# Seven-product pairs in the second round of both FFN down projections, and a weight stream that loads by free tiles

## The chip, the cores and the metric

The kernel runs on one core of one Trainium2 chip. The metric is the device time of one execution in microseconds (us), as the median of three runs. Engines are called as the profile calls them: PE (TensorE matmul), PEld (its weight loads), DVE (VectorE), ACT (ScalarE), POOL (GpSimd), SP (SyncE, which here only issues DMAs).

## The reference, cut to what matters

The program is a two-layer decoder trunk over 512 tokens of width 1024: a Mamba-2 layer, an FFN, a latent attention layer, a second FFN, with a layer norm after each of the four. The change sits in the FFN, which runs twice:

```python
def conv_ffn(h, up, conv_w, conv_b, down):
    u = causal_depthwise_conv(h @ up, conv_w, conv_b)
    g, val = jnp.split(u, 2, axis=-1)
    return (jax.nn.silu(g) * val) @ down
...
        h = layer_norm(DN_ALPHA * h + mix, ln_mix_g[i], ln_mix_b[i])
        ff = conv_ffn(h, ffn_up[i], ffn_conv_w[i], ffn_conv_b[i], ffn_down[i])
        h = layer_norm(DN_ALPHA * h + ff, ln_ffn_g[i], ln_ffn_b[i])
```

`up` is 1024 x 5632 and `down` 2816 x 1024, both float32. The hidden width of 2816 is 22 tiles of 128.

## The kernel before

**Precision.** Every large product is made of three float32r matmuls: each operand is split into a rounded part and a remainder (`h` and `l`), and hh, hl and lh are added up in PSUM (`mm_a` for the up projection, lines 148, `mm_b` for the down projection, lines 154 to 156). A weight tile therefore goes through three steps before PE can use it: a DMA into a staging tile `wst`, a cast on ACT into `wh` (line 84), and a subtraction on DVE into `wl` (line 85). The last two are called a split here. An item of the stream is one such tile, 128 x 1024 (wide) or 128 x 512 (narrow).

**The weight stream.** `WStream` walks a list of items made ahead of time. There are 3 staging tiles and 6 pairs of `wh` and `wl`. `get(i)` splits items up to 4 ahead of `i`, never more than 6 beyond the last item retired; after each split the stream issues loads until 3 items past the split are loaded. SP issues its DMAs in the written order; a DMA whose staging tile is still in use holds up those behind it. DVE and ACT also take their instructions in a fixed order, made by a scheduler from program order and its own estimate.

**The FFN** (function `ffn`) works in two rounds over the hidden tiles. Round 0 takes tiles 0 to 9, round 1 tiles 10 to 21. A round first makes its hidden tiles: for each tile 48 matmuls (gate and value), then convolution, silu, gate on ACT and DVE (`conv3_silu_gate`). Then it multiplies them by their rows of `down`:

- Round 0 takes the tiles in pairs of an even and an odd one (`down_pairs`). With two halves of the tokens and two halves of the output columns, one pair is a 2 x 2 by 2 x 2 block product, which is done with seven block products in place of eight. `pair_operands` makes the four sums of hidden tiles on DVE; the sums of the weights are made in three `sums` tiles (`rs`, `rs2`). The item kinds say how: "r" loads into the sum, "a" is a DMA from POOL that adds to it, "+" adds a staged tile to it on DVE (line 78), "=" uses that same staged tile by itself, "-" subtracts a staged tile from the sum (line 81). The seven products run in the order a11, s1, then s2 and s4 alternating, s3, a12, a22, into PSUM banks X, Y and Z (two banks each, one for each of two token tiles). After a product, `add` moves its banks into the residual `h` on DVE (line 341), since X and Y are used again.
- The five pairs of round 0 are cut into parts of two, two and one pairs, one item for each part: 21 items a round.
- Round 1 takes its 12 tiles in the plain way: for the first half of the columns all four token tiles at once over 6 wide items, then for the second half one token tile after the other over 6 more, with the layer norm of a token tile behind its last product. In the last FFN the last token tile's second half is made in two quarters, so that its layer norm (`ln_last`) starts early.

The layer norm's parameters (`lngb`, 1 MB) share their place with the sums, and are loaded by SP after round 0.

Of the kernel before, what the change touches and what calls it, by code (L numbers as in the profile page):

```python
# [18 lines left out]
P = 128  # L19
# [11 lines left out]
class WStream:  # L31
    def __init__(self, k, items, nb, nst, la):
        self.k, self.items, self.nb, self.nst, self.la = k, items, nb, nst, la
        self.loaded = 0
        self.split = 0
        self.done = 0
        self.st = {}
        self.w = {}

    def _load(self):  # L40

        i = self.loaded
        src, f, kind, part = (self.items[i] + (None, None))[:4]
        if kind == "=":
            self.st[i] = self.st[i - 1]
            self.loaded += 1
            return  # L50
        if kind in ("r", "a"):
            t = self.sums[part]
            v = t[:, :f].rearrange("p (a n) -> p a n", a=src.shape[1])
            if kind == "r":
                self.k.nc.sync.dma_start(v, src)
            else:
                self.k.nc.gpsimd.dma_start(v, src, accum_op=ALU.add)
            self.st[i] = t
            self.loaded += 1
            return  # L60
        t = self.k.wst.tile([P, 1024], F32, name="wst")
# [3 lines left out]
        self.k.nc.sync.dma_start(dst, src)  # L65
        self.st[i] = t
        self.loaded += 1

    def _split(self, nst=None):
        nc = self.k.nc  # L70
        i = self.split
        while self.loaded <= i:
            self._load()
        f, kind, part = (self.items[i][1:] + (None, None))[:3]
        s = self.st.pop(i)
        if kind == "+":
            r = self.sums[part]
            nc.vector.tensor_tensor(r[:, :f], r[:, :f], s[:, :f], op=ALU.add)
            s = r
        elif kind == "-":  # L80
            nc.vector.tensor_tensor(s[:, :f], self.sums[part][:, :f], s[:, :f], op=ALU.subtract)
        h = self.k.wh.tile([P, 1024], F32R, name="wh")
        l = self.k.wl.tile([P, 1024], F32R, name="wl")
        nc.scalar.copy(h[:, :f], s[:, :f])  # L84
        nc.vector.tensor_tensor(l[:, :f], s[:, :f], h[:, :f], op=ALU.subtract)  # L85
        self.w[i] = (h, l)
        self.split += 1
        while self.loaded < min(len(self.items), self.split + (self.nst if nst is None else nst)):
            self._load()
# [17 lines left out]
class K:  # L107
    def __init__(self, tc, ctx, nb=6, nst=3, la=4):
        self.tc, self.nc, self.ctx = tc, tc.nc, ctx
        nc = self.nc  # L110
        self.nb, self.nst, self.la = nb, nst, la
        pool = lambda n, b, **kw: ctx.enter_context(tc.tile_pool(name=n, bufs=b, **kw))

        self.small = pool("small", 1)
        self.const = pool("const", 1)
        self.hp = pool("hp", 1)
        self.htp = pool("htp", 1)
        self.wst = pool("wst", nst)
# [12 lines left out]
        self.st = {}  # L131
# [114 lines left out]
R0 = 10  # L246


def ffn_items(up, down):


    it = []
    dv = down.rearrange("(k p) n -> p k n", p=P)
    for r in range(2):
        ks = range(R0) if r == 0 else range(R0, HT)
        for c in ks:
            it.append((up[c], 1024))
            it.append((up[c + HT], 1024))
        if r:
            for hf in range(2):  # L260
                for j in range(R0, HT, 2):
                    it.append((dv[:, j:j + 2, hf * 512:(hf + 1) * 512], 1024))
            continue

        def b(odd, hf, j):
            n = min(4, R0 - j)
            return dv[:, j:j + n, hf * 512:(hf + 1) * 512].rearrange("p (k e) n -> p k e n", e=2)[:, :, odd, :], n * 256

        for odd, hf, kinds in ((0, 0, "r"), (0, 1, "a"), (1, 1, "+="), (0, 0, "-"), (1, 0, None), (1, 0, "a")):
            for p, j in enumerate(range(0, R0, 4)):  # L270
                for kind in kinds or (None,):
                    it.append(b(odd, hf, j) + (kind, p))
# [43 lines left out]
def down_pairs(k, ws, n, prs):  # L316
# [6 lines left out]
    ni = (len(prs) + 1) // 2  # L323
    seen = set()

    def product(bs, op, p, i, start, stop):
        wh, wl = ws.get(i)
        ps = prs[2 * p:2 * p + 2]
# [8 lines left out]
    def add(bs, row, hf, sign):  # L337
        for t in range(2):
            i = 2 * row + t
            hs = k.h[:, i, hf * 512:(hf + 1) * 512]  # L340
            last = nc.vector.scalar_tensor_tensor(hs, hs, 1.0 if (i, hf) in seen else ALPHA, bs[t], op0=ALU.mult,  # L341
                                                  op1=ALU.add if sign > 0 else ALU.subtract)
            seen.add((i, hf))
# [29 lines left out]
def ffn(k, ws, base, cwp, gb, la=2, out=None, mid=None):  # L373

    nc, tc = k.nc, k.tc
    with ExitStack() as c:
# [6 lines left out]

        rs = k.lnp.tile([P, 2, DM], F32, name="rs", tag="lngb")
        ws.sums = [rs[:, 0], rs[:, 1], pools["rs"].tile([P, 512], F32, name="rs2")]
        new_gt = lambda: pools["gt"].tile([P, 2, SEQ], F32R, name="gt")
        for r in range(2):
            gts, prs, half = [], [], {}

            def finish(ci, bg, bv):  # L390
                if r:
# [7 lines left out]
                j = ci // 2  # L399
# [43 lines left out]
            for hf in range(2):  # L443
                final = hf == 1
                nk = HT - R0
                if not final:
                    bs = [k.bank() for _ in range(NT)]
                    for j in range(0, nk, 2):
                        wh, wl = ws.get(n)
                        for jj in range(2):  # L450
                            for i in range(NT):
                                k.mm_b(bs[i], gts[j + jj], slice(i * P, (i + 1) * P), wh[:, jj * 512:(jj + 1) * 512],
                                       wl[:, jj * 512:(jj + 1) * 512], j + jj == 0, j + jj == nk - 1)
                        ws.retire(n)
                        n += 1
                    ws.ahead(n)
                    for i in range(NT):
                        k.add_mix(i, hf, bs[i], 1.0, True)
                else:
                    if out is None:  # L460
                        k.new_ht()
                    def piece(i, b, c0, c1, retire):
                        for jc in range(6):
                            wh, wl = ws.get(n + jc)
                            for jj in range(2):
                                j = jc * 2 + jj
                                o = slice(jj * 512 + c0, jj * 512 + c1)
                                k.mm_b(b, gts[j], slice(i * P, (i + 1) * P), wh[:, o], wl[:, o], j == 0, j == nk - 1)
                            if retire:
                                ws.retire(n + jc)  # L470

                    for i in range(NT):
                        if out is not None and i == NT - 1:
                            bs = [k.bank(), k.bank()]
                            for e in range(2):
                                piece(i, bs[e][:, :256], e * 256, e * 256 + 256, e == 1)
                            k.ln_last(i, [v[:, :256] for v in bs], out[i * P:(i + 1) * P, :])
                            continue
                        b = k.bank()
                        piece(i, b, 0, 512, i == NT - 1)  # L480
                        if i == NT - 1:
                            ws.ahead(n + 6, la)
                        k.add_mix(i, hf, b, 1.0, True)
                        if out is None and i:
                            k.transpose_h(i - 1)
                        k.ln_apply(i)
                        if out is not None:
                            for f in range(2):
                                fs = slice(f * 512, (f + 1) * 512)
                                nc.sync.dma_start(out[i * P:(i + 1) * P, fs], k.h[:, i, fs])  # L490
                    n += 6
# [31 lines left out]
def ssd(k, ws, base, xT, x, cwp, hv, ngp, gb):  # L523
    nc, tc = k.nc, k.tc
    with ExitStack() as cx:
# [28 lines left out]
        ws.loaded = 1  # L554
        for a, e in XT:
# [6 lines left out]
            elif e < KT:  # L562
                ws._load()
# [729 lines left out]
def trunk_kernel(tc, *aps):  # L1293
    d = dict(zip(_INS, aps))
    out = aps[len(_INS)]
    with ExitStack() as ctx:
# [6 lines left out]
        ws = WStream(k, items, k.nb, k.nst, k.la)  # L1303
# [57 lines left out]
```

## Time and profile before

| what | value |
|---|---|
| median of 3 runs | 1334.68 us (1333.44 to 1335.08) |
| the profiled execution | 1332.25 us, of which its span is 1330.5 us |
| granted PE clock | 0.999 |
| first FFN: up of round 0, its products, up of round 1, its down | from 434.3, 535.8, 585.1, 715.7 to 782.8 us |
| second FFN: the same stages | from 976.1, 1077.6, 1126.8, 1257.3 to 1323.0 us |
| DMA traffic | 140.39 MB, mean 106 GB/s |

The profile shows one execution. Its span is the time from the first to the last instruction; some 1.8 us of the execution lie around it. Instruction rows give the start, the duration, engine, line and the tiles, then in brackets how long the engine sat idle before and what released it. Matmuls are pipelined, so the duration of one is longer than the time from its start to the next one's.

### The profile page before, as it was taken

To read this page: it belongs to the slowest core of one execution; us is meant where nothing else is said; L and a number is where in the kernel's file an instruction comes from. 1 tells how busy PE (TensorE), PEld (TensorE's weight loads), DVE (VectorE), ACT (ScalarE), POOL (GpSimd) and SP (SyncE) were. 2 spreads that over 40 slices of the span, in tenths; PEclk is the share of its full clock that TensorE was granted. 3 is DMA by queue.
4 is the path that set the end of the run, shared out by engine and by line. 5 is a ranking of instruction groups with operands and counts; after the bars stand their busy time and mean duration, and the time that the engine had idled before them with its cause. 6 is when DMAs were issued, how large, how long until landed. Compare 5 with 4: busy or idle time off the path is not lost.

```text
span 1330.5 us, 17374 instructions
## 1 busy us (share of the span) xinstructions
PE 1317.7 (99%) x6794; PEld 1114.5 (84%) x6794; DVE 945.3 (71%) x1433; ACT 616.7 (46%) x988; POOL 88.9 (7%) x86
## 2 busy tenths in 40 slices
PE   9999999999999999999999999999999999999997
PEld 8888888888888988788888899888898887888886
DVE  7788898788798877766664366888577786565534
ACT  6665555546443544344443144665254443444411
POOL 0111011001012001000000022000100100000001
PEclk9999999999999999999999999999999999999999
DMA  7433422332321443452223222311053426333211
GB/s 245 177 111 112 127 93 98 112 126 69 123 96 51 137 139 66 109 200 96 95 95 108 67 90 66 94 48 64 32 162 95 122 50 197 137 99 100 101 49 64
DMA packets 47186, 140.39 MB, mean 106 GB/s; under 512 B 4960, under 2 KB 5984, under 8 KB 45568
## 3 DMA queue, kind: packets, MB, share of 16 engines
q1 hardware_dynamic: 44352, 134.04, 30.5%
q0 software_dynamic: 2752, 5.24, 2.3%
q8 instruction: 53, 0.87, 0.3%
q14 instruction: 29, 0.24, 0.1%
HBM read 137.10 MB, written 2.16 MB: 105 GB/s over the span
## 4 chain that ended last, share of the span: by engine, by line
PE 95%; DVE 2%; DMA 2%; issue 1%; ACT 0%; SPq 0%; DVEq 0%; ACTq 0%
PE ps L148 57%; PE ps L154 9%; PE ps L156 9%; PE ps L155 9%; PE ps L1181 2%; PE ps L731 1%; PE ps L1215 1%; DMA wst<-in_down_dram 1%; PE ps L739 1%; DVE wl L85 1%; PE ps L234 1%; PE ps L720 1%; PE ps L698 1%; PE ps L1202 1%; PE ps L839 1%; PE ps L672 1%
## 5 line engine op out<-in xcount | busy, mean ns | idle before, releaser
L148 PE MATMUL ps<-ht,wh 128*128 128x512 f32 (+1 forms) x2272 | 518.8, 379 | 0.7 <-ACT ht L237 0.4
L148 PEld LDWEIGHTS ps<-ht,wh 128*128 128x128 f32 x2272 | 409.1, 188 | 79.8 <-ACT ht L237 0.8
L85 DVE TENSOR_TENSOR wl<-wst,wh 128x1024 fp32r<-128x1024 f32 (+3 forms) x220 | 259.8, 1188 | 99.0 <-ACT wh L84 98.7
L84 ACT CAST wh<-wst 128x1024 fp32r<-128x1024 f32 (+3 forms) x220 | 222.7, 1018 | 163.5 <-PE ps L156 88.8
L148 PE MATMUL ps<-ht,wl 128*128 128x512 f32 (+1 forms) x1136 | 267.4, 378 | 0.0
L148 PEld LDWEIGHTS ps<-ht,wl 128*128 128x128 f32 x1136 | 206.0, 188 | 39.4
L154 PE MATMUL ps<-wh,gt 128*128 128x512 f32 (+1 forms) x344 | 131.8, 383 | 2.6 <-DVE h L341 2.6
L155 PE MATMUL ps<-wl,gt 128*128 128x512 f32 (+1 forms) x344 | 131.4, 382 | 0.0
L156 PE MATMUL ps<-wh,gt 128*128 128x512 f32 (+1 forms) x344 | 131.4, 382 | 0.0
L283 DVE SCALAR_TENSOR_TENSOR acc<-ps,cw,acc 128x511 f32<-128x511 f32 x88 | 65.7, 746 | 88.6 <-ACT acc L282 88.6
L587 DVE SCALAR_TENSOR_TENSOR cv<-ps,cw,cv 128x511 f32<-128x511 f32 (+2 forms) x96 | 71.2, 744 | 34.1 <-ACT cv L585 33.5
L282 ACT ACTIVATE acc<-ps,cw 128x512 f32<-128x512 f32 x88 | 68.3, 776 | 36.8 <-PE ps L148 36.8
L295 ACT CAST gt<-acc 128x512 fp32r<-128x512 f32 (+1 forms) x64 | 36.9, 586 | 97.2 <-DVE acc L288 95.4
L154 PEld LDWEIGHTS ps<-wh,gt 128*128 128x128 f32 x344 | 64.7, 188 | 15.8 <-DVE h L341 3.5
L156 PEld LDWEIGHTS ps<-wh,gt 128*128 128x128 f32 x344 | 64.7, 188 | 12.5
L155 PEld LDWEIGHTS ps<-wl,gt 128*128 128x128 f32 x344 | 64.7, 188 | 12.4
L284 DVE SCALAR_TENSOR_TENSOR acc<-ps,cw,acc 128x510 f32<-128x510 f32 x88 | 65.8, 748 | 2.7
L287 ACT ACTIVATE acc<-acc 128x512 f32<-128x512 f32 x44 | 27.8, 632 | 82.7 <-DVE acc L284 82.4
L296 DVE TENSOR_TENSOR gt<-acc,gt 128x512 fp32r<-128x512 f32 (+1 forms) x64 | 40.9, 647 | 18.9 <-ACT gt L295 18.9
L690 ACT ACTIVATE W<-W,cum 128x128 f32<-128x128 f32 x128 | 41.0, 392 | 23.4 <-DMA W<-cumd 23.4
L154 PE MATMUL ps<-wh,yT 128*128 128x512 f32 x128 | 50.9, 397 | 0.0
L686 POOL TENSOR_TENSOR CE<-CE,cv 128x1536 f32<-128x1536 f32 x8 | 28.6, 3575 | 326.2 <-ACT CE L685 326.2
(240 smaller groups left out, 1646.4 us busy)
## 6 DMA issues: line engine op xcount, KB each, us to landing
wst<-in_up_dram SPq DMA_DIRECT2D x88, 512.0 KB, 3.4
wst<-in_down_dram SPq DMA_DIRECT2D x36, 512.0 KB, 3.6
wst<-in_xbc_dram SPq DMA_DIRECT2D x32, 512.0 KB, 4.2
W<-cumd SPq DMA_DIRECT2D x8, 1024.0 KB, 4.6
wst<-in_sow_dram SPq DMA_DIRECT2D x16, 512.0 KB, 3.5
wst<-in_zw_dram SPq DMA_DIRECT2D x14, 512.0 KB, 3.5
lngb<-in_gb_dram SPq DMA_DIRECT2D x4, 1024.0 KB, 5.7
rs<-in_down_dram POOLq DMA_DIRECT2D x8, 512.0 KB, 6.6
```

What stands on the lines that cost most here:

```text
L84: nc.scalar.copy(h[:, :f], s[:, :f])
L85: nc.vector.tensor_tensor(l[:, :f], s[:, :f], h[:, :f], op=ALU.subtract)
L148: nc.tensor.matmul(out, w[:, k, :], xts[k][:, x, ts], start=first and p == 0 and k == 0, stop=last and p == 2 and k == nk - 1, skip_group_ ...
L154: nc.tensor.matmul(out, xt[:, 0, tsl], wh, start=start, stop=False, skip_group_check=True)
L155: nc.tensor.matmul(out, xt[:, 0, tsl], wl, start=False, stop=False, skip_group_check=True)
L156: nc.tensor.matmul(out, xt[:, 1, tsl], wh, start=False, stop=stop, skip_group_check=True)
L282: nc.scalar.activation(a, b, AF.Identity, bias=cw[:, ch, 3:4], scale=cw[:, ch, 2:3])
L283: nc.vector.scalar_tensor_tensor(a[:, 1:], b[:, :SEQ - 1], cw[:, ch, 1:2], a[:, 1:], op0=ALU.mult, op1=ALU.add)
L284: nc.vector.scalar_tensor_tensor(a[:, 2:], b[:, :SEQ - 2], cw[:, ch, 0:1], a[:, 2:], op0=ALU.mult, op1=ALU.add)
L296: k.nc.vector.tensor_tensor(dst[:, 1, :], src, dst[:, 0, :], op=ALU.subtract)
L587: nc.vector.scalar_tensor_tensor(t[:, d:], b[:, :SEQ - d], cw[:, ch, 3 - d:4 - d], t[:, d:], op0=ALU.mult, op1=ALU.add)
L690: nc.scalar.activation(w, w, AF.Relu, bias=D["cum"][:, c, g * HPG + h:g * HPG + h + 1], scale=-1.0)
```

## The change

Round 1 now takes its tiles 10 to 15 as three pairs with seven products, in parts of one pair each (21 narrow items, 126 matmuls of 512 columns), after all 12 of its hidden tiles are made. The other six tiles go through a loop over token tiles: for each, both column halves one after the other over the same six wide items, then its layer norm. The three-pair stage adds to the residual with factor 1, since round 0 has applied ALPHA.

The stream has six staging tiles instead of three within the FFNs (three count elsewhere), and issues loads whenever a staging tile is free in its count; loads into the sums are issued as soon as their sum isn't in use by an earlier item. `down_pairs` asks for splits three items ahead instead of four. The build reserves 4096 (not the default) for the scratch of dynamically issued DMAs, which makes room for the three tiles. `lngb` is loaded after round 1's pairs.

```diff
+    def fill(self, nst=None):
+        used = set()
+        for i in range(self.split, min(len(self.items), self.split + self.nb + self.nst)):
+            kind, part = (self.items[i][2:] + (None, None))[:2]
+            if i not in self.st and kind != "=":
+                if kind in ("r", "a"):
+                    if part not in used:
+                        self.load(i)
+                elif self.out < (self.nst if nst is None else nst):
+                    self.load(i)
+                else:
+                    break
+            if kind:
+                used.add(part)
...
-    def __init__(self, tc, ctx, nb=6, nst=3, la=4):
+    def __init__(self, tc, ctx, nb=6, nst=6, la=4):
...
-R0 = 10
+RP = ((2, 2, 1), (1, 1, 1))
+R0 = 2 * sum(RP[0])
+R1 = R0 + 2 * sum(RP[1])
...
-        wh, wl = ws.get(i)
-        ps = prs[2 * p:2 * p + 2]
+        wh, wl = ws.get(i, 3)
+        ps = prs[at[p]:at[p + 1]]
...
-            if not r:
-                if mid:
-                    mid()
-                n = down_pairs(k, ws, n, prs)
-                k.load_ln(gb)
...
+            if mid and not r:
+                mid()
+            n = down_pairs(k, ws, n, prs, RP[r], not r)
+        k.load_ln(gb)
...
+        for i in range(NT):
+            last = i == NT - 1
+            b = k.bank()
+            piece(i, b, 0, 0, 512, last)
+            k.add_mix(i, 0, b, 1.0, True)
+            if out is not None and last:
+                bs = [k.bank(), k.bank()]
+                for e in range(2):
+                    piece(i, bs[e][:, :256], 1, e * 256, e * 256 + 256, e == 1)
+                k.ln_last(i, [v[:, :256] for v in bs], out[i * P:(i + 1) * P, :])
                 continue
+            b = k.bank()
+            piece(i, b, 1, 0, 512, last)
+            if last:
+                ws.ahead(n + 2 * nw, la)
+            k.add_mix(i, 1, b, 1.0, True)
...
-    nc = _bacc.Bacc("TRN2", target_bir_lowering=False, num_devices=1)
+    nc = _bacc.Bacc("TRN2", target_bir_lowering=False, num_devices=1, dynamic_dma_scratch_size=4096)
```

The change moves instructions on DVE and SP. Three places matter for what follows. In the rows, a name's number tells buffers apart: ps_4851 and ps_4852 are the banks X, ps_4853 and ps_4854 the banks Y of round 0 before.

First, DVE in round 0 of the first FFN, where the products s2 and s4 end and s3 is to start in the banks X. Before:

```order
L85 TENSOR_TENSOR wl_5007<-wst_4954,wh_5006 128x1024
L85 TENSOR_TENSOR wl_5026<-wst_4972,wh_5025 128x512
L341 SCALAR_TENSOR_TENSOR h_93<-h_93,ps_4851 128x512
L85 TENSOR_TENSOR wl_5038<-wst_4991,wh_5037 128x1024
L341 SCALAR_TENSOR_TENSOR h_93<-h_93,ps_4852 128x512
L341 SCALAR_TENSOR_TENSOR h_93<-h_93,ps_4853 128x512
L341 SCALAR_TENSOR_TENSOR h_93<-h_93,ps_4854 128x512
L85 TENSOR_TENSOR wl_5053<-wst_5010,wh_5052 128x1024
```

The same place now (X is ps_4861 and ps_4862, Y ps_4863 and ps_4864; line 97 is the old 85, line 352 the old 341):

```order
L97 TENSOR_TENSOR wl_5026<-wst_4688,wh_5025 128x1024
L97 TENSOR_TENSOR wl_5040<-wst_4743,wh_5039 128x512
L352 SCALAR_TENSOR_TENSOR h_93<-h_93,ps_4861 128x512
L352 SCALAR_TENSOR_TENSOR h_93<-h_93,ps_4862 128x512
L352 SCALAR_TENSOR_TENSOR h_93<-h_93,ps_4863 128x512
L352 SCALAR_TENSOR_TENSOR h_93<-h_93,ps_4864 128x512
L97 TENSOR_TENSOR wl_5057<-wst_4912,wh_5056 128x1024
```

The split that stood between the two adds of X (wl_5038, the first item of product a12) now stands behind all four adds.

Second, DVE in round 1 of the first FFN, from the end of product a11 to the start of s4 (X is ps_6143 and ps_6144, Y ps_6145 and ps_6146; lines 88 and 91 are the "+" and "-" operations; gt_6130 is the last hidden tile). Nothing of this stood there before:

```order
L298 TENSOR_TENSOR acc_6135<-acc_6131,acc_6135 128x512
L352 SCALAR_TENSOR_TENSOR h_93<-h_93,ps_6143 128x512
L352 SCALAR_TENSOR_TENSOR h_93<-h_93,ps_6144 128x512
L306 TENSOR_TENSOR gt_6130<-acc_6135,gt_6130 128x512
L88 TENSOR_TENSOR rs_3893<-rs_3893,wst_5760 128x512
L91 TENSOR_TENSOR wst_5980<-rs_3893,wst_5980 128x512
L97 TENSOR_TENSOR wl_6175<-rs_3893,wh_6174 128x512
L97 TENSOR_TENSOR wl_6179<-wst_5760,wh_6178 128x512
L97 TENSOR_TENSOR wl_6198<-rs_3893,wh_6197 128x512
L352 SCALAR_TENSOR_TENSOR h_93<-h_93,ps_6145 128x512
L352 SCALAR_TENSOR_TENSOR h_93<-h_93,ps_6146 128x512
L97 TENSOR_TENSOR wl_6210<-wst_5833,wh_6209 128x512
```

Between the adds of X (product a11) and those of Y (product s1) stand six other operations.

Third, SP at the end of round 1 of the first FFN, where `lngb` is now loaded (in_dw_dram is the first weight of the attention layer):

```order
L54 DMA wst_6294<-in_down_dram 128x2x512
L54 DMA wst_6300<-in_down_dram 128x2x512
L54 DMA wst_6318<-in_down_dram 128x2x512
L54 DMA wst_6364<-in_dw_dram 128x1024
L54 DMA wst_6370<-in_dw_dram 128x1024
L54 DMA wst_6388<-in_dw_dram 128x1024
L54 DMA wst_6402<-in_dw_dram 128x1024
L54 DMA wst_6408<-in_dw_dram 128x768
L172 DMA lngb_6410<-in_gb_dram 128x2048
L54 DMA wst_6424<-in_dw_dram 128x768
```

It stood among the first loads of round 1's up projection before; now it stands behind five loads of the next layer, each of which waits for a staging tile.

More of the change, by code (lines that the diff above doesn't have):

```diff
@@ L38, in __init__, with load @@
         self.w = {}
[L40 to L61, printed above, removed]
+    def load(self, i):
+        src, f, kind = (self.items[i] + (None,))[:3]
+        t = self.sums[self.items[i][3]] if kind in ("r", "a") else self.k.wst.tile([P, 1024], F32, name="wst")
         dst = t[:, :f]
@@ L81, in _split @@
             nc.vector.tensor_tensor(s[:, :f], self.sums[part][:, :f], s[:, :f], op=ALU.subtract)
+        if kind not in ("r", "a", "+"):
+            self.out -= 1
         h = self.k.wh.tile([P, 1024], F32R, name="wh")
@@ L313, in pair_operands, with down_pairs @@
     split(k, s34, v)
-def down_pairs(k, ws, n, prs):
+def down_pairs(k, ws, n, prs, parts, first):
     nc = k.nc
     X, Y, Z = ([k.bank() for _ in range(2)] for _ in range(3))
-    ni = (len(prs) + 1) // 2
-    seen = set()
+    ni = len(parts)
+    at = [sum(parts[:p]) for p in range(ni + 1)]
+    new = {(i, hf) for i in range(NT) for hf in range(2)} if first else set()
     def product(bs, op, p, i, start, stop):
-        wh, wl = ws.get(i)
-        ps = prs[2 * p:2 * p + 2]
+        wh, wl = ws.get(i, 3)
+        ps = prs[at[p]:at[p + 1]]
         for t in range(2):
@@ new lines, in ffn @@
+        for i in range(NT):
[8 more added lines that the diff above has]
+                k.ln_last(i, [v[:, :256] for v in bs], out[i * P:(i + 1) * P, :])
+                continue
+            b = k.bank()
[3 more added lines that the diff above has]
+            k.add_mix(i, 1, b, 1.0, True)
+            if out is None and i:
+                k.transpose_h(i - 1)
+            k.ln_apply(i)
+            if out is not None:
+                for f in range(2):
+                    fs = slice(f * 512, (f + 1) * 512)
+                    nc.sync.dma_start(out[i * P:(i + 1) * P, fs], k.h[:, i, fs])
```

119 lines of the change are left out of this document (44 added, 75 removed).

## The prediction

> **What bounds the kernel now.** I read the page first, then the waits of PE, then the busy times by stage.
>
> ```profile
> span 1330.5 us, 17374 instructions
> PE 1317.7 (99%) x6794; PEld 1114.5 (84%) x6794; DVE 945.3 (71%) x1433; ACT 616.7 (46%) x988; POOL 88.9 (7%) x86
> ...
> PE ps L154 <- DVE h L341: 2.6, 2, 1.4
> ```
>
> PE is never out of work for long. Its largest wait is the last row: 2.6 us in two places, one in each FFN, for the add that empties a bank of the seven products. So time can be won in two ways only: fewer matmuls, or those 2.6 us. The stages say what a matmul costs (columns: stretch, its length, then PE, PEld, DVE, ACT, POOL busy with counts, clock, DMA share, GB/s):
>
> ```profile
> 434.30:535.60 101.30, 101.30 (x506) 86.41 (x505) 79.52 (x121) 48.72 (x69) 3.49 (x3) 1.00 0.39 112
> 535.80:585.10 49.30, 47.95 (x211) 39.38 (x211) 37.00 (x47) 21.71 (x26) 3.28 (x3) 1.00 0.51 143
> 585.10:715.60 130.50, 130.50 (x577) 108.14 (x577) 78.07 (x95) 55.10 (x70) 0.00 (x0) 1.00 0.34 113
> ...
> 1077.60:1126.70 49.10, 47.83 (x211) 39.31 (x210) 36.78 (x47) 21.56 (x26) 3.29 (x3) 1.00 0.50 146
> ...
> 1314.46 0.28 PE L154 MATMUL ps<-wh,gt 128*128 128x256 f32 x1
> ...
> 1322.97 0.28 PE L156 MATMUL ps<-wh,gt 128*128 128x256 f32 x1
> ```
>
> The third row is round 1's up projection: 130.50 us, always busy. Its 576 matmuls of 512 columns start 0.2266 us apart (130.50/576). The rows of 256 columns are the first and last of 72 in the last token tile: (1322.97 - 1314.46)/71 = 0.1199 us. In the seven-product stages of rows 2 and 4, 211 matmuls would take 47.81 us at that spacing; they take 49.30 and 49.10, so 1.5 and 1.3 us are lost, 2.8 together (the waits gave 2.6). The granted clock is 1.00 in every row.
>
> **The change part by part.** *Fewer matmuls.* A pair costs 48 matmuls of 512 columns plainly and 42 with seven products. Three pairs save 18 in the first FFN: 18 x 0.2266 = **4.08 us**. In the second, round 1's down goes from 252 of 512 and 72 of 256 columns to 252 and 36: 36 x 0.1199 = **4.32 us**. Sum 8.4 us, all on PE's path.
>
> [...]
>
> *The stall in round 0.* The chain of waits around 564 us, and DVE's rows there:
>
> ```profile
> 555.58 7.28 DMA wst<-in_down_dram
> ...
> 562.96 1.06 ACT wh L84
> ...
> 565.19 0.69 DVE h L341
> ...
> 565.92 0.50 PE ps L154
> ...
> 552.59 0.69 DVE L85 TENSOR_TENSOR wl<-wst,wh 128x512 fp32r<-128x512 f32 x1
> 553.20 1.22 DVE L81 TENSOR_TENSOR wst<-rs,wst 128x1024 f32<-128x1024 f32 x1
> 554.33 1.23 DVE L85 TENSOR_TENSOR wl<-wst,wh 128x1024 fp32r<-128x1024 f32 x1
> ...
> 561.21 0.69 DVE L341 SCALAR_TENSOR_TENSOR h<-h,ps 128x512 f32<-128x512 f32 x1 [1.67 <-PE ps L156]
> 564.05 1.23 DVE L85 TENSOR_TENSOR wl<-wst,wh 128x1024 fp32r<-128x1024 f32 x1 [2.15 <-ACT wh L84]
> 565.19 1.88 DVE L341 SCALAR_TENSOR_TENSOR h<-h,ps 128x512 f32<-128x512 f32 x3
> ```
>
> DVE made the first add of X at 561.21, then stood before a split whose tile landed late (a load of 7.28 us, started at 555.58 because only three staging tiles exist), and made the second add of X at 565.19. PE needed X for s3. In the new order that split stands behind all four adds, so the load can't hold them; it also takes the staging tile that the first "=" split gives back, and no longer one of three. I take the 2.8 us as gone; lower bound 2.6, the waits' row.
>
> *What the new stage asks of DVE.* Durations in round 0's products, and the start of such a stage:
>
> ```profile
> L84 ACT CAST wh<-wst 128x512 fp32r<-128x512 f32 x3 | 1.9, 618 | 1.8 <-DVE wst L81 1.8
> L85 DVE TENSOR_TENSOR wl<-wst,wh 128x512 fp32r<-128x512 f32 x3 | 2.1, 685 | 0.0
> L341 DVE SCALAR_TENSOR_TENSOR h<-h,ps 128x512 f32<-128x512 f32 x13 | 8.6, 686 | 4.8 <-PE ps L156 4.8
> ...
> 535.85 0.39 PE L154 MATMUL ps<-wh,gt 128*128 128x512 f32 x1
> 536.87 0.75 DVE L283 SCALAR_TENSOR_TENSOR acc<-ps,cw,acc 128x511 f32<-128x511 f32 x1 [1.49 <-ACT acc L282]
> ...
> 538.91 0.69 DVE L288 TENSOR_TENSOR acc<-acc 128x512 f32<-128x512 f32 x1
> ```
>
> Back to back, a 512-column operation starts 0.6 us after the one before (552.59 to 553.20) and a wide one 1.13 us (553.20 to 554.33). PE's time for the new stage is 126 x 0.2266 = 28.55 us, 1.36 us an item. DVE has 21 splits, 3 "+", 3 "-" and 14 adds, 41 x 0.6 = 24.6 us, and the rest of the last gate before it. It is close, so I walk down DVE's order with t = 0 at the first matmul of a11.
>
> The gate's product ends at 3.75 (538.91 + 0.69 - 535.85). X's adds start at 3.8 and 4.4; gate split 5.0; "+" 5.6; "-" 6.2; the sum's cast (0.62) ends at 6.95; three splits at 7.0, 7.6, 8.2; Y's adds at 8.8 and 9.4, ending 9.5 and 10.1. s4 needs Y's first bank at 8.16 + 1.36 = 9.52, its second at 10.2. **That is the tightest place, with no margin.** Then: second and third part's operations and the "-" splits until 15.0; X's adds to 16.3, Y's to 17.5. s3 needs X at 16.33 and 17.0: margin 0.6. The loads of a12 start when "=" tiles come free at 8.3, 10.7 and 13.3; with the 7.28 us of the chain the last lands at 20.6 and is split by 22.0, needed at 23.1. Of the six wide items the tightest has 1.4 us. After the first, small shortfall each deadline is met.
>
> I take 0.3 us of waiting at Y for each FFN, 0.6 in all; its bounds are 0 and the 1.4 us of the old wait, the nearest row, each. The cover is that walk; without it the adds of Y go late one for one.
>
> *The accumulating DMAs and `lngb`.* The stage adds three transfers on POOL before s1 and three before a22.
>
> ```profile
> L57 POOL DMA_DIRECT2D rs<-in_down_dram x12 | 13.4, 1119 | 241.8 <-DVE wl L85 174.6 <-ACT wh L84 60.5 <-issue 4.4
> ...
> 552.61 1.19 POOL L57 DMA_DIRECT2D rs<-in_down_dram  x1 [30.25 <-ACT wh L84]
> 554.96 1.19 POOL L57 DMA_DIRECT2D rs<-in_down_dram  x1 [1.15 <-DVE wst L81]
> ...
> rs<-in_down_dram POOLq DMA_DIRECT2D x1, 256.0 KB, 7.5
> ...
> lngb<-in_gb_dram SPq DMA_DIRECT2D x4, 1024.0 KB, 5.7
> ...
> 764.86 0.69 DVE L174 SCALAR_TENSOR_TENSOR h<-h,ps 128x512 f32<-128x512 f32 x1 [2.55 <-PE ps L156]
> ...
> 767.54 1.42 DVE L188 SCALAR_TENSOR_TENSOR h<-h,lnst,lngb 128x512 f32<-128x512 f32 x2 [0.34 <-ACT lnjunk L183]
> 769.40 1.41 DVE L191 SCALAR_TENSOR_TENSOR h<-h,lnst,lngb 128x512 f32<-128x512 f32 x2 [0.44 <-POOL lnst L185]
> ```
>
> The sums are read for the last time at 7.7, 8.9 and 12.7; the last transfer lands by 12.7 + 1.1 + 7.5 = 21.3, DVE reaches it at 23.2, PE at 27.2: hidden. `lngb` in the first FFN now waits on SP behind loads whose fifth staging tile comes free at about 32.3, and lands at 38.4 with the 5.7 us row. Queued behind it are one load of the next layer and, on DVE, the norm of token tile 0. That norm needs it 2.7 us after the tile's last product (764.86 to 767.54, the product being just over), at 39.3, and PE wants the normed tile only one tile later (8.16 us), 2 to 3 us after the norm ends. Cost 0; if it came over 3 us later, PE would wait that excess once.
>
> *The end.* The last token tile's norm starts from quarters half as long:
>
> ```profile
> 1320.16 0.42 DVE L205 SCALAR_TENSOR_TENSOR h<-h,ps 128x256 f32<-128x256 f32 x1
> ...
> 1322.12 0.15 DVE L210 TENSOR_SCALAR lnst<-lnlast 128x1 f32<-128x1 f32 x1 [0.85 <-ACT lnjunk L208]
> 1323.29 0.42 DVE L211 SCALAR_TENSOR_TENSOR h<-h,ps 128x256 f32<-128x256 f32 x1 [1.02 <-PE ps L156]
> ```
>
> L205 already waited for DVE's earlier norm, not for PE. One more add (0.7) goes ahead of it, which moves L210 to 1322.8, still ahead of L211; L211 itself is bound to PE's end. Cost 0, bounds 0 and 0.2. Making the pairs' sums in round 1's up stage is round 0's work again: the first row of the stages has it with PE busy 101.30 of 101.30, so its cover holds. Three more staging tiles cost nothing on an engine.
>
> Sum: 4.08 + 4.32 + 2.8 - 0.6 = 10.6 us. The profiled execution (1332.25 us) would go to 1321.65, the median shown (1334.68), which is 2.4 us above it, to **1324.1 us**.
>
> **Rivals.** (1) *DVE paces the new stage.* If each of its 41 operations costs its full 0.686 us and not 0.6, it ends 3.5 us later; 1.1 us of margin absorb a part, 2.4 us reach PE in each FFN: 1324.1 + 4.8 = 1328.9. For it: 37.00 us of DVE in 49.30 in round 0, and no margin at Y. Against it: the starts 0.6 us apart.
>
> (2) *The stall moves instead of going* (the six staging tiles are still taken in turn, and SP's loads in written order): the 2.8 us stay, 1326.9. Against it: the four adds now stand together.
>
> (3) *The accumulating transfers go one after another, and the kernel is slower than before.* In the stage, three of them each of 0.9 + 7.5 us after 7.7 land at 32.9; with cast and split (1.3) the last item of a22 is ready at 34.2 and needed at 27.2: 7.0 us in each FFN, 1324.1 + 14.0 = 1338.1. It makes the change a loss once a transfer takes over 7.8 us in the row of three. For it: the scratch of dynamic DMAs is cut to 4096, and no row shows what that limits; six loads share the engines. Against it: the issues at 552.61 and 554.96 lie closer than one landing, so such transfers overlap now.
>
> [...]
>
> **How the numbers follow.** Forecast 0.62 (1322 to 1327 with its bounds and the spread of the three runs), rival 1 0.19, rival 2 0.07, rival 3 0.05, a mix of small losses that eats nearly all 0.07. The range from 1321.5 (no new wait and a run 1.2 us low, as the lowest shown) to 1330.0 holds the first three but for the tail of rival 1. Within 0.2% means 2.7 us, about what a measurement of this kernel can tell from no change: faster is below 1332.0 and has 0.87, same 0.07, slower 0.06.
>
> **What would show it.** In the profile after, round 1's down stage should be 18 matmuls shorter, with PE's waits for L352 (the old L341) under 1 us in all, none of them at s3 of round 0. A wait of PE at the first s4 of round 1 by more than 0.5 us is rival 1; a wait of ACT for the sums after a POOL transfer is rival 3. Wrong would be a matmul spacing other than 0.2266 us, or waits in the attention layer from its earlier loads, which I took as free.

## The result, and the profile after

| | before | after |
|---|---|---|
| median of 5 runs | 1334.68 us (1331.74 to 1335.89) | 1320.27 us (1319.76 to 1320.59) |
| the profiled execution | 1332.25 us, span 1330.5 | 1320.28 us, span 1318.6 |
| from the start to the last matmul | 1322.97 us | 1311.21 us |

The changed kernel takes 0.9898 of the time before (95% interval 0.9884 to 0.9911). That is 3.8 us under the forecast of 1324.1 and 1.2 us under its range. The profiled execution fell by 12.0 us and the median by 14.4: the two kernels differ not only in their time but in how far their runs lie apart, 4.2 us before and 0.8 after.

The page of after, its span, PE's busy time and the chain of work that ended last:

```profile
span 1318.6 us, 17522 instructions
PE 1309.1 (99%) x6740; PEld 1106.3 (84%) x6740; DVE 998.0 (76%) x1539; ACT 633.1 (48%) x1030; POOL 99.9 (8%) x98
...
PE 98%; DVE 1%; issue 0%; ACT 0%; DVEq 0%; ACTq 0%
```

There are 54 matmuls less than before (6794 to 6740), and DVE has 106 operations more, 53 us of busy time. Next PE's waits, all that are left, with what each waited for, us in total, times and longest:

```profile
PE ps L554 <- DVE warm L135: 1.1, 1, 1.1
PE ps L1183 <- DVE qrT L1171: 0.5, 1, 0.5
PE ps L159 <- ACT ht L248: 0.4, 1, 0.4
PE ps L159 <- DVE ht L249: 0.3, 1, 0.3
PE ps L1183 <- DVE kT L1159: 0.2, 1, 0.2
```

The largest row of before, 2.6 us for the add of the seven products, has no successor: no row has line 352. The stages (stretch, length, then PE, PEld, DVE, ACT, POOL busy with counts, clock, DMA share, GB/s), in order the products of round 0, the up projection of round 1, the new three-pair stage in the first FFN, and the same in the second:

```profile
534.80:582.60 47.80, 47.80 (x212) 39.60 (x211) 37.01 (x47) 21.81 (x26) 3.28 (x3) 1.00 0.49 147
582.60:713.20 130.60, 130.60 (x577) 108.16 (x577) 84.92 (x116) 55.11 (x76) 2.57 (x3) 1.00 0.29 88
713.20:741.90 28.70, 28.70 (x128) 23.58 (x126) 25.84 (x39) 15.78 (x23) 2.60 (x3) 1.00 0.60 173
...
1249.74:1278.40 28.66, 28.66 (x127) 23.55 (x126) 25.78 (x39) 15.83 (x23) 2.61 (x3) 1.00 0.64 202
```

PE is busy in every microsecond of all four. Round 0's products take 47.80 us, where they took 49.30; the up projection keeps its 130.6 us with 21 more DVE operations beside it; the new stage takes 28.7 us, and its 126 matmuls at 0.2267 us make 28.56. DVE is busy for 25.84 of its 28.70 us, 90%, and PE doesn't wait for it.

DVE where s3 is to start in round 0, which showed the stall before:

```profile
557.71 0.69 DVE L97 TENSOR_TENSOR wl<-wst,wh 128x512 fp32r<-128x512 f32 x1 [0.68 <-ACT wh L96]
560.41 2.73 DVE L352 SCALAR_TENSOR_TENSOR h<-h,ps 128x512 f32<-128x512 f32 x4 [2.01 <-PE ps L167]
563.06 2.96 DVE L97 TENSOR_TENSOR wl<-wst,wh 128x1024 fp32r<-128x1024 f32 x3
```

The four adds follow one another, and DVE waits only for PE ahead of them; the splits come behind.

### The profile page after: what moved, and what is told of

Same layout as the page of the kernel before. It is cut to its first block, busy times and chain, and to the rows that moved or that the text cites. A ratio compares the mean times of both kernels' runs of the same rounds, so it can differ in the third digit from the quotient of the medians.

```text
span 1318.6 us, 17522 instructions
## 1 busy us (share of the span) xinstructions
PE 1309.1 (99%) x6740; PEld 1106.3 (84%) x6740; DVE 998.0 (76%) x1539; ACT 633.1 (48%) x1030; POOL 99.9 (8%) x98
## 4 chain that ended last, share of the span: by engine, by line
PE 98%; DVE 1%; issue 0%; ACT 0%; DVEq 0%; ACTq 0%
PE ps L159 57%; PE ps L165 10%; PE ps L167 10%; PE ps L166 10%; PE ps L1183 2%; PE ps L733 1%; PE ps L1217 1%; PE ps L841 1%; PE ps L741 1%; PE ps L245 1%; PE ps L722 1%; PE ps L700 1%; PE ps L1204 1%; PE ps L674 1%; DVE wl L97 0%; PE ps L554 0%
## 5 line engine op out<-in xcount | busy, mean ns | idle before, releaser
L97 DVE TENSOR_TENSOR wl<-wst,wh 128x1024 fp32r<-128x1024 f32 (+4 forms) x226 | 254.9, 1145 | 38.3 <-ACT wh L96 38.0
L96 ACT CAST wh<-wst 128x1024 fp32r<-128x1024 f32 (+4 forms) x226 | 219.9, 984 | 94.3 <-PE ps L167 48.8
L165 PE MATMUL ps<-wh,gt 128*128 128x512 f32 (+1 forms) x326 | 125.9, 386 | 0.0
L167 PE MATMUL ps<-wh,gt 128*128 128x512 f32 (+1 forms) x326 | 125.6, 385 | 0.0
L166 PE MATMUL ps<-wl,gt 128*128 128x512 f32 (+1 forms) x326 | 125.6, 385 | 0.0
L305 ACT CAST gt<-acc 128x512 fp32r<-128x512 f32 (+1 forms) x76 | 42.3, 574 | 101.9 <-DVE acc L298 98.8
L165 PEld LDWEIGHTS ps<-wh,gt 128*128 128x128 f32 x326 | 61.2, 188 | 12.7 <-issue 0.5
L167 PEld LDWEIGHTS ps<-wh,gt 128*128 128x128 f32 x326 | 61.2, 188 | 12.2
L52 POOL DMA_DIRECT2D rs<-in_down_dram x24 | 23.8, 991 | 567.3 <-DVE wl L97 434.4
L96 ACT CAST wh<-rs 128x512 fp32r<-128x512 f32 (+1 forms) x48 | 36.6, 763 | 46.7 <-DVE rs L88 23.3
L306 DVE TENSOR_TENSOR gt<-acc,gt 128x512 fp32r<-128x512 f32 (+1 forms) x76 | 46.8, 631 | 14.0 <-ACT gt L305 14.0
L352 DVE SCALAR_TENSOR_TENSOR h<-h,ps 128x512 f32<-128x512 f32 x56 | 36.9, 684 | 21.7 <-PE ps L167 21.7
```

The source lines that it names most:

```text
L165: nc.tensor.matmul(out, xt[:, 0, tsl], wh, start=start, stop=False, skip_group_check=True)
L166: nc.tensor.matmul(out, xt[:, 0, tsl], wl, start=False, stop=False, skip_group_check=True)
L167: nc.tensor.matmul(out, xt[:, 1, tsl], wh, start=False, stop=stop, skip_group_check=True)
L305: k.nc.scalar.copy(dst[:, 0, :], src)
L306: k.nc.vector.tensor_tensor(dst[:, 1, :], src, dst[:, 0, :], op=ALU.subtract)
```

## The experiments

Two questions were open: which part of the change brings what, and why the median fell more than the profiled execution. All kernels were timed beside runs of the kernel before on the same chip; those runs gave medians of 1333.66, 1332.60 and 1333.57 us in three sets.

### The kernel before, three more times

No edit; three more profiles, the first with timed runs.

> The kernel before, unchanged, with a second profile. Theory A (the stall in round 0 has another length in each execution, since the load that ends it lands earlier or later; the profile of before caught a short one): median near 1334.7 us, runs spread over 3 to 4 us, and a second profile in which the two stalls of PE (once in each FFN, before the product s3) add up to another length than the 3.2 us of the first, with the profiled time moving by the same amount. Theory B (the distance between the profiled execution and the median belongs to the chip or the measurement): the same median and spread, but stalls of 3.2 us again however long the execution is, and the difference spread over the program.

> The kernel before once more, for one more profile. Theory A: where the profiled time is over 1334 us, the stalls before s3 are longer than the 1.7 us of the two profiles so far (2.5 to 4 us, or followed by matmuls 0.43 us apart), behind a load of more than 7.3 us; where it is near 1332 us, they are 1.6 to 1.8 us again. Theory B: a slow profile has stalls of 1.7 us too, and its time is lost elsewhere.

> The same once more, with the same expectation: stalls before s3 that grow with the profiled time (theory A), or that stay at 1.7 us (theory B).

The second profile, at 1331.57 us, had stalls like the first's (3.1 us against 3.2) and so couldn't tell the two theories apart; the timed runs of e1 gave 1333.29 us (1331.55 to 1335.88), 0.9996 of before (0.9986 to 1.0005). The other two were at 1334.68 and 1333.33 us. First the one at 1334.68, at s3 in the second FFN: its chain of waits (start, length, what).

```profile
1097.44 7.93 DMA wst<-in_down_dram
...
1105.46 1.06 ACT wh L84
...
1107.68 0.69 DVE h L341
...
1108.42 0.50 PE ps L154
```

PE's rows at the same place, in its timeline (start, duration, engine, line, tiles, then how long it was idle and what released it):

```profile
1106.04 0.39 PE L156 MATMUL ps<-wh,gt 128*128 128x512 f32 x1
1108.42 0.50 PE L154 MATMUL ps<-wh,gt 128*128 128x512 f32 x1 [1.99 <-DVE h L341]
...
1109.22 0.63 PE L154 MATMUL ps<-wh,gt 128*128 128x512 f32 x1
1109.65 0.63 PE L155 MATMUL ps<-wl,gt 128*128 128x512 f32 x1
...
1112.63 0.39 PE L156 MATMUL ps<-wh,gt 128*128 128x512 f32 x1
```

And the 4 us behind the stall in the busy times by stretch, where the third column from the end is the granted clock:

```profile
1109.00:1113.00 4.00, 4.00 (x12) 3.15 (x11) 2.74 (x4) 2.51 (x3) 0.00 (x0) 0.57 0.33 127
```

The load took 7.93 us here, not 7.28; PE stood for 2.38 us from start to start, not 1.74; and behind it eight matmuls start 0.43 us apart in place of 0.23. The granted clock over those 4 us is 0.57. So this late load costs its own lateness and then 8 x 0.2 = 1.6 us of slower matmuls.

All four profiles can be put into one account. "Start" is the time at which the first wide products of the program reach the same matmul (the 242nd of each profile); "s3" is what the starts of PE's matmuls behind the stall lie further apart than 0.2267 us, in the first and the second FFN; "rest" is everything else up to the last matmul, "tail" what comes behind its start:

| profile | execution | span | start | s3, first | s3, second | rest | tail |
|---|---|---|---|---|---|---|---|
| before, first | 1332.25 | 1330.54 | 45.21 | 1.63 | 1.54 | 1274.60 | 7.57 |
| before, e1 | 1331.57 | 1329.85 | 44.61 | 1.53 | 1.59 | 1274.55 | 7.57 |
| before, e12 | 1333.33 | 1331.63 | 45.09 | 1.64 | 2.19 | 1275.14 | 7.58 |
| before, e11 | 1334.68 | 1332.98 | 44.87 | 1.49 | 3.86 | 1275.17 | 7.58 |
| order alone, e2 | 1329.44 | 1327.73 | 44.82 | 0 | 0 | 1275.32 | 7.59 |
| stream alone, e3 | 1329.83 | 1328.12 | 45.64 | 0 | 0 | 1274.92 | 7.56 |
| after | 1320.28 | 1318.56 | 44.44 | 0 | 0 | 1266.78 | 7.35 |

The executions of before differ by 3.1 us, and 2.2 of these are s3. Over 50 timed runs of before the time goes with the granted clock of the whole execution: 14 runs at 0.999 have a mean of 1332.6 us, 21 at 0.998 1333.3, 12 at 0.997 1334.6, and 3 at 0.996 1336.5; the median of all is 1333.57. Theory A holds for the profiles: the one from which I took the price of the stall was one of the two cheap ones. That the slowest timed runs lost their time in such stalls too is inferred from their clock, as no trace of them was kept. The start moves too, by up to 1.2 us over these profiles, in kernels of the old stream and of the new.

### The order alone

```diff
-        wh, wl = ws.get(i)
+        wh, wl = ws.get(i, 3)
```

> The kernel before with one edit: the seven products ask for splits three items ahead, not four. On DVE the split that stood between the two adds of X moves behind all four adds; loads, staging tiles and the plain second round stay. Theory A: the stalls go and with them their whole mean length, so 1334.7 - 4 to 5.5 = 1329 to 1331 us, with a spread under 1.5 us. Theory B: 2.8 to 3.2 us less, 1331.5 to 1332, with the spread of before. Third possibility (the order only moves the wait, since a12's load still starts late with three staging tiles): 1333 to 1335, with a wait of PE at the first item of a12 instead.

Measured 1328.91 us (1328.08 to 1329.44), 0.9967 of before (0.9955 to 0.9979). PE has no wait at s3 in either FFN. One number in the kernel before is worth 4.75 us against the median of its runs, and takes the spread from 4.8 to 1.4 us. The wait did not move to a12.

### The stream alone

The class `WStream` of after, its six staging tiles and the small scratch, put into the kernel before, with splits three ahead as well; the second round stays plain.

```diff
-    def __init__(self, tc, ctx, nb=6, nst=3, la=4):
+    def __init__(self, tc, ctx, nb=6, nst=6, la=4):
...
-        wh, wl = ws.get(i)
+        wh, wl = ws.get(i, 3)
...
+        ws.nst = k.nst
```

> The new weight stream, six staging tiles and splits three ahead, but the plain second round of before (no pairs there). Theory A: after's time plus the 8.4 us that the pairs save, 1328.7 us, spread under 1.5 us, no stall before s3. Theory B: 1334.7 - 3.2 = 1331.5 us. If the start of the program gains from the staging tiles, its zdt matmuls show none of the two gaps of 0.71 and 0.40 us, and 0.8 us of the difference to the kernel with the order alone lie there.

Measured 1329.13 us (1328.14 to 1329.83), 0.9969 of before (0.9958 to 0.9981): as much as the order alone, which it contains. The gain at the start did not come: its two gaps are here again, and the start is the latest of the table. From here to after it is 8.86 us by the medians, which is the pairs; these two medians come from different sets of runs.

### The pairs alone

The three pairs with the kernel before's stream, its three staging tiles, splits four ahead and its scratch.

```diff
-R0 = 10
+RP = ((2, 2, 1), (1, 1, 1))
+R0 = 2 * sum(RP[0])
+R1 = R0 + 2 * sum(RP[1])
```

> The three pairs of the second round alone: the weight stream of before, three staging tiles, splits four ahead, the default scratch. Theory A and B both: 8.4 us from the matmuls, 1334.7 - 8.4 = 1326.3 us, with the stall and the spread of before in round 0. More than 1327.5 would mean that the second round's pairs need the new stream (waits of PE in the three-pair stage); less than 1324.5 would mean that the pairs save more than their matmuls, and the stall less than I now think.

Measured 1338.56 us (1336.68 to 1340.50), 1.0039 of before (1.0026 to 1.0051): **slower by 0.4%**, where I had expected 1326.3 us. The pairs took their matmuls away and gave back more than that in their own stage and right behind it. DVE there, in the first FFN:

```profile
730.59 0.69 DVE L341 SCALAR_TENSOR_TENSOR h<-h,ps 128x512 f32<-128x512 f32 x1 [0.28 <-PE ps L156]
734.80 0.69 DVE L81 TENSOR_TENSOR wst<-rs,wst 128x512 f32<-128x512 f32 x1 [3.52 <-DMA wst<-in_down_dram]
735.41 1.28 DVE L341 SCALAR_TENSOR_TENSOR h<-h,ps 128x512 f32<-128x512 f32 x2
```

The busy times of the stretches there, with the granted clock third from the end:

```profile
733.00:740.00 7.00, 4.13 (x12) 3.09 (x11) 4.29 (x7) 1.66 (x3) 0.86 (x1) 0.76 0.62 163
740.00:752.00 12.00, 12.00 (x55) 9.91 (x54) 10.80 (x14) 6.40 (x8) 0.00 (x0) 1.00 0.70 234
```

It is round 0's stall again, only longer: between the adds of X stands a subtraction whose staged tile landed 3.5 us late, and the granted clock is 0.76 over the 7 us that hold PE's wait and the matmuls behind it, 1.00 over the next 12. The gaps beyond 0.2267 us are 5.8 us in this stage with the token tile behind it, and 6.9 in the second FFN's. The stall of round 0 is there too, and shows once more that it goes with the load (the chain of waits at s3 of the first FFN):

```profile
555.16 8.16 DMA wst<-in_down_dram
...
566.38 0.50 PE ps L154
```

0.88 us more of load than in before's first profile (7.28), and a gap of 2.61 us in place of 1.74, 0.87 more.

### One part undone at a time

Three kernels between the pairs alone and after. First after with splits four ahead:

```diff
-        wh, wl = ws.get(i, 3)
+        wh, wl = ws.get(i)
```

> The changed kernel with one part undone: the seven products ask for splits four items ahead again, so that the first split of a12 stands between the two adds of X in round 0, as before. Six staging tiles and loads by free tiles stay. If the stall needs both that place and a late load (the tile of that split is now loaded several us earlier), no stall comes back: 1320.3 us, within 0.7, spread under 1.5 us. If the place alone makes it, 1320.3 + 4.75 = 1325 us with a spread of 4 us. In the three-pair stage each split stands one item earlier, which may cost the adds 0 to 1 us in each FFN.

Measured 1320.76 us (1320.74 to 1321.02), 0.9906 of before (0.9892 to 0.9919). DVE at s3 of round 0:

```profile
561.22 0.69 DVE L352 SCALAR_TENSOR_TENSOR h<-h,ps 128x512 f32<-128x512 f32 x1 [2.01 <-PE ps L167]
561.82 1.22 DVE L97 TENSOR_TENSOR wl<-wst,wh 128x1024 fp32r<-128x1024 f32 x1
562.96 1.88 DVE L352 SCALAR_TENSOR_TENSOR h<-h,ps 128x512 f32<-128x512 f32 x3
```

The split stands between the adds of X just as before, and it costs nothing: it runs right behind the first add, as its load was issued at 546.5 us and not at 555.6, and had landed at 550.0. The stall needs both, the place and the late load; each half of the change removes it by itself.

Then after with its count of staging tiles set to three, and the pairs alone with splits three ahead:

```diff
-        ws.nst = k.nst
+        ws.nst = 3
```

> The changed kernel with three staging tiles in use within the FFNs in place of six, all else as changed (loads by free tiles, splits three ahead). Round 0 should stay free of the stall before s3, as with the order alone. If the six tiles are what feeds the three-pair stage, the waits of the run with the pairs alone come back there (a wait of 3 us or more for a staged tile of the minus splits, then matmuls at half the clock): 1330 to 1336 us. If the place of the splits or the order of the loads feeds it, 1320 to 1322 us.

> The run with the pairs alone (1338.56 us) with splits three ahead: old stream, three staging tiles, three pairs in the second round. Round 0's stall goes, 4.75 us: 1333.8 us if the three-pair stage keeps its waits of about 14 us; 1320 to 1322 if the place of the splits was the cause there too.

The first gave 1320.85 us (1320.46 to 1320.94), 0.9905 of before (0.9890 to 0.9920), and no wait in the three-pair stage. But it doesn't test the number of tiles, as I had meant it to. The edit lowers only the count that `fill` goes by; the pool still hands out six buffers in turn. SP's loads for the three-pair stage and the six wide tiles behind it, in after (start, length, what, how many):

```profile
655.91 76.95 SPq L54 DMA_DIRECT2D wst<-in_down_dram  x15
```

The same in this run, where the whole stage comes 0.65 us later:

```profile
656.56 76.94 SPq L54 DMA_DIRECT2D wst<-in_down_dram  x15
```

And in the pairs alone with splits three ahead, whose stage starts at 713.2 us like that of after:

```profile
673.37 71.51 SPq L65 DMA_DIRECT2D wst<-in_down_dram  x15
```

With each tile counted from the issue of its load to the end of its split, up to six are out at a time in this run as in after, and outside the FFNs too, where both kernels set the count to three; in the FFNs of the old stream there are never more than three. So this run repeats after in this stage.

The old stream with splits three ahead gave 1326.29 us (1325.52 to 1328.27), 0.9948 (0.9936 to 0.9961), between the two times that I had expected: of the 18.3 us between the pairs alone and after, 12.3 come from the place of the splits, and 6.0 are left. PE's gaps in its two three-pair stages and the token tile behind each add up to 6.9 us; two rows of its waits:

```profile
PE ps L155 <- DVE wl L85: 2.3, 8, 0.5
...
PE ps L154 <- ACT wh L84: 0.8, 1, 0.8
```

Both are split tiles that come late. What is left belongs to the new stream as a whole, the rule by which it issues loads together with its six buffers. No run takes these two apart, so which of them the stage needs stays open.

### Four pairs

```diff
-RP = ((2, 2, 1), (1, 1, 1))
+RP = ((2, 2, 1), (2, 1, 1))
```

> The changed kernel with four pairs in the second round (parts of two, one and one pair) and four plain tiles. Six matmuls of 512 columns less in each FFN, 12 x 0.2266 = 2.7 us: 1317.6 us if the new stage keeps up as with three pairs. If DVE or the loads are at their limit there, waits of PE before s4 or s3 of that stage, and 1319 to 1324 us.

A miss: 1328.23 us (1327.24 to 1328.63), 0.9959 of before (0.9947 to 0.9972), slower than after by 8 us. The pair stage itself keeps up; the loss is behind it. PE's largest wait:

```profile
PE ps L245 <- DVE h L202: 3.7, 2, 2.7
```

The chain of waits there, behind the pair stage of the first FFN:

```profile
756.11 7.83 DMA lngb<-in_gb_dram
764.04 0.81 DVE h L199 x2
764.85 0.52 issue
765.37 0.76 DVE h L202
766.17 1.97 PE ps L245 x8
```

With four plain tiles left, a token tile takes 24 matmuls, 5.4 us, and the layer norm can no longer hide: `lngb`, issued at 756.1 us behind loads of the next layer where after has 746.1, lands late in the first FFN, and the work behind the last matmul at the program's end grows from 7.35 to 11.08 us. Between the two profiles 4.4 us are lost in the first FFN from its pair stage on, 3.7 at the end and 1.2 in the start, against 1.6 us that the second FFN gains. Four pairs are one too many here.

### A stall of known length

After, with 6 or 9 DVE operations ahead of the adds of X in round 0, which read X and write a tile that nothing uses:

```diff
+    if first:
+        dl = k.junk[0].tile([P, 512], F32, name="delay", tag=k.junk[1])
+        for q in range(6):
+            nc.vector.tensor_scalar(dl, X[q % 2], 1.0, 1.0, op0=ALU.mult, op1=ALU.mult)
     add(X, 0, 1, -1)
```

> The changed kernel with six extra DVE operations that read the banks X in round 0, put ahead of the adds of X that s3 waits for: 5 x 0.69 us more before the first bank is free, of which 1.4 us or so are margin, so PE stands some 2 us before s3, once in each FFN. The matmul spacing behind the stall stays 0.2267 us, and the time is after's 1320.3 + 4 = 1324.3 us, with a spread under 1.5 us (the stall is made by DVE alone and no load decides it).

> The same with nine operations: PE stands some 5 us before s3 in each FFN. Theory A (a stall over about 3 us also halves PE's clock for some us behind it, as in the run with the pairs alone, so the long stalls among before's executions cost more than their length): 1320.3 + 10 + 2 x 2 to 2.7 = 1334.3 to 1336, with matmuls 0.43 us apart behind each stall. Without that: 1330.3 us.

The short one gave 1327.30 us (1326.93 to 1328.65), 3 us over what I expected, and the long one 1333.32 us (1332.05 to 1334.68). The short one's gap was 2.25 us in both FFNs, but behind the first seven matmuls ran 0.43 us apart and behind the second none: 3.73 and 2.13 us lost for the same gap. The long one's gaps of 4.42 us were both followed by matmuls 0.43 us apart, 5.8 and 5.9 us lost. The long one's time lies between the 1330.3 us without slow matmuls and the 1334.3 to 1336 of theory A. Theory A's limit of about 3 us, an estimate from the pairs alone (slow matmuls behind gaps of 3.26 and 3.89 us, none behind one of 2.61), was too high: one gap of 2.25 us here cost 3.73 us. What it said of the stretch behind a stall, matmuls 0.43 us apart, came behind three of the four gaps of these two runs.

## Why the prediction came out as it did

**Fewer matmuls (8.4 us): right.** In the account the rest falls from 1274.5 to 1275.3 (six profiles with the plain round) to 1266.78, 8.2 us from their mean, and the tail by 0.2; the medians from the stream alone to after, of different sets, give 8.86.

**The stall goes (2.8 us): the mechanism right, the size wrong.** It went for the reason given, the split behind the adds, and the order alone shows that this suffices. But 2.8 us were read from one execution, with a load of 7.28 us, and the load is not the same each time. In the four profiles of before s3 costs 3.2, 3.1, 3.8 and 5.4 us, and by medians the order alone brings 4.75.

**The offset of 2.4 us is the step that failed.** I put the forecast 2.4 us above the profiled execution, because the median of before lay there, as if that distance belonged to the chip and would stay. Most of it was the stall: its long cases, and the slow matmuls behind them. By the medians the order alone is worth 4.75 us, 1.6 us more than the 3.17 that s3 cost in the first profile. The other 0.8 us no trace explains; the median of 1334.68 stands on few runs, and that of the 50 later ones is 1333.57. When the stall goes, the distance goes: the profiled execution of after is its median. Of the 3.8 us that the forecast was off, 2.4 are this step. The remaining 1.4 lie in the sum for the profiled execution (1321.65 against 1320.28): 0.6 us for a wait that didn't come, 0.4 us of s3, 0.8 us of a start that happened to be early and 0.2 us of tail, less 0.6 us by which the rest fell short of 8.4. The spread of 1333.4 to 1335.1 in the three runs, with a profile at 1332.25, was the sign I had in hand: something in the program had a length that changed. That widened my range by 1.2 us; it should have moved the forecast. The range has a slip of its own: the two terms named for its lower end, no new wait (0.6 us) and a run 1.2 us low, give 1322.3 us and not 1321.5.

**New waits at Y's adds (0.6 us): did not come.** DVE at that place in round 1, with the first matmul of a11 at 713.21:

```profile
716.88 1.30 DVE L352 SCALAR_TENSOR_TENSOR h<-h,ps 128x512 f32<-128x512 f32 x2
718.10 0.69 DVE L306 TENSOR_TENSOR gt<-acc,gt 128x512 fp32r<-128x512 f32 x1
718.70 0.69 DVE L88 TENSOR_TENSOR rs<-rs,wst 128x512 f32<-128x512 f32 x1
719.42 0.69 DVE L91 TENSOR_TENSOR wst<-rs,wst 128x512 f32<-128x512 f32 x1
720.13 0.69 DVE L97 TENSOR_TENSOR wl<-rs,wh 128x512 fp32r<-128x512 f32 x1
720.74 0.69 DVE L97 TENSOR_TENSOR wl<-wst,wh 128x512 fp32r<-128x512 f32 x1
721.34 0.69 DVE L97 TENSOR_TENSOR wl<-rs,wh 128x512 fp32r<-128x512 f32 x1
721.94 1.28 DVE L352 SCALAR_TENSOR_TENSOR h<-h,ps 128x512 f32<-128x512 f32 x2
```

The walk had Y's adds at 8.8 and 9.4; they start at 8.73 and 9.33. It held to 0.1 us, no margin was indeed next to no wait (PE loses 0.1 us there), and the 0.3 us that I added for each FFN was a surcharge on a walk that needed none. Rival 1, with each operation at its full 0.69 us, was wrong: most start 0.6 us apart here too, two of them 0.7.

**The accumulating DMAs (0): right.** No wait of PE or ACT behind them; L52 takes 0.99 us on average for 24, less than L57's 1.12 us for 12, and the three of the first FFN's new stage landed 4.7 to 6.0 us after their issue, where I had taken 7.5. Rival 3 did not happen. **`lngb` (0 at PE): right, by a narrow cover.** What waited for it, and its time to landing, in the view of that tile:

```profile
  DVE h L199: 2.5, 1
...
DMA to landing us min/median/max: 7.5/7.5/7.5
```

It took 7.5 us and not 5.7, landed at 753.6 us, 40.4 after the stage's start where I had 38.4, and held DVE for 2.5 us; that is inside the 3 us which I gave as the cover, and PE didn't notice. The four pairs show the other side of this limit.

**Rival 2 (the stall only moves): no**, in after. It is what the pairs alone did, where the wait in the new stage is the same one. I had not seen that the pairs lose by themselves: without the new stream, and with splits four ahead, the new stage and the token tile behind it lose more than the pairs save.

## What to carry to other kernels

The stall that ended with a DMA had a distribution here, not a length: s3 cost 1.49 to 3.86 us over the four profiles of before, behind loads of 7.15 and 7.93 us for these two (both in e11). Where the runs scatter by more than the rest of the program explains, take the stall's price from several profiles, and expect its removal to bring the spread down with the median (here from 4.8 to 1.4 us). Look at which instruction stands behind a late load in an in-order queue: moving the load (e5) or moving the instruction (e2) each left PE without a wait at s3 here, and for round 0's stall one number did what the whole new stream did. Work that saves matmuls only pays if its supply keeps up; the same three pairs cost 4.9 us with the old stream and its splits four ahead, and saved 8.9 us with the new one.

## What the runs showed of the hardware

PE's matmuls ran slower behind stalls shorter than I had thought. Gaps from start to start of 1.61 to 1.76 us (s3 in the profiles of before) were never followed by matmuls 0.43 us apart; of gaps between 2.25 and 2.61 us two of five were (2.25 in e9's first FFN and 2.38 in e11's second yes; 2.25 in e9's second, 2.30 in e12's second and 2.61 in e4's first no); gaps of 3.07 us (e8), 3.26 and 3.89 (e4) and twice 4.42 (e10) all were. The slow stretch lasted for eight matmuls in e11 and seven in e9, and cost up to some 2.6 us (e4, second FFN). The busy times around e11's gap of 2.38 us, with the granted clock third from the end:

```profile
1105.00:1109.00 4.00, 2.01 (x10) 1.34 (x9) 2.46 (x4) 1.05 (x1) 0.00 (x0) 1.00 0.94 262
1109.00:1113.00 4.00, 4.00 (x12) 3.15 (x11) 2.74 (x4) 2.51 (x3) 0.00 (x0) 0.57 0.33 127
1113.00:1117.00 4.00, 4.00 (x20) 3.28 (x19) 2.66 (x4) 1.68 (x2) 0.00 (x0) 1.00 0.68 253
```

The granted clock was 1.00 over the 4 us in which PE stood idle for 1.99 and started again at 1108.42, 0.57 over the next 4 and 1.00 after that. Why one gap of 2.25 us in e9 cost 3.73 us and the other 2.13, in the same execution, was not shown.

What makes the load of 512 KB at s3 of the first FFN take 7.15 us in one execution (e11) and 8.16 in another (e4) was not tried and stays open.
